# S5 stage of a two-block kernel: turned states kept on their rows, table tiles of 64 rows, decays and U factors made one by one

## The chip, the cores and the metric

The kernel runs on one core of one Trainium2 chip. The metric is device time in microseconds (us) of one execution, as the median of several runs. The profile is one execution of the same program, recorded by the hardware; its times are us from the start of the span unless they are marked ns.

## The reference

Two blocks follow each other on 512 tokens of 1024 features: a block of a convolution and pooling mixer ("even") and a gated linear recurrence ("odd"), then a block of an S5 state-space mixer, an MLP, a gated projection and windowed attention. The part at hand is the S5 mixer. Each of 64 groups has 16 channels and 64 complex states:

```python
a = exp((lam_re + i lam_im) * dt)                      # per group and state
x[t] = a * x[t-1] + B u[t]                             # complex recurrence
y[t] = Re(C x[t]) + d * u[t]                           # C c_re, c_im
y = gelu(y);  ab = y @ w_glu;  out = ab[:, :1024] * sigmoid(ab[:, 1024:])
```

## The kernel before

The S5 mixer works on 64 chunks of 8 tokens. Inside a chunk everything is matrix products with tables; between chunks there is a scan over 64 columns. The features lie in eight tiles (`ft` 0 to 7) of eight groups each.

**Tables.** `tables` makes four tables for each tile while the even stage runs (80 to 430 us), a piece at each `tick`, and writes them to DRAM: `tS` (inputs to states), `tO` (states to outputs), `tM` (inputs to outputs inside a chunk) and `tR` (cosine C and sine N of the rotation of each chunk). `stored` (L1076 to L1080) puts `tO` out with four transfers of 64 rows on SP's queue for each of 16 half tiles.

**odd_out** (L813) ends the odd stage. For each of eight feature tiles it adds the residual (DVE), turns the columns (ACT, `r`), sends them through DRAM by two transfers on POOL's queue into `U`, and then makes two squares (ACT) that are added up (DVE) for two norms.

**s5** (L1165). `enter(ft)` loads the tables S, O, M0, `rotations` loads R; all on SP's queue. `fillers(n)` are blocks of an independent projection, six matmuls of 512 columns each, that are put between; `FILL` says how many stand at which place: four blocks, then the column sums of the squares (`columns`, L368), two blocks, then a chain of small DVE operations (reciprocal square root, three Newton steps, `sel`), 16 small matmuls (L1208) that spread the factor, and one block. Then four decay tiles `dec` (128x512) are made on POOL, U of tiles 0 and 1 is multiplied by the factor on DVE, and U of tiles 2 to 7 on POOL.

- `states(ft)`: 16 matmuls S by U into the PSUM bank `sp` (L1262, 128 rows by 64 columns, two instructions each), then on DVE: multiply by C (512 wide), by N (two of 256), add and subtract (two of 256), two scans of 256 (L1277), multiply by C again (512), by N again (two of 256), a small memset, and four operations on 64 rows by 252 that put real and imaginary part of the turned states `e` on other rows.
- `leave(ft)`: for each of the eight groups, two matmuls M by U (L1302) and two matmuls O by e (L1304), each 128 rows by 64 columns; Gelu on ACT, a round trip through DRAM (`dy`, `yc`), and the split into two halves for the matmuls of `glu`.

The order on PE is the order of the program: states(1) is issued before leave(0), and so on: leave(ft), one block, states(ft+2). From tile 5 on, after each leave, two pieces (`part`, three matmuls each) of the first GLU products follow. `with self.after()` ties a block behind the last instruction of PE issued so far; DVE's states are tied one behind the other (`SEQ`). On the other engines a planner sets the order by a simulated timeline. The weights of `glu` come as `raw` by SP's queue into two buffers, are split by ACT (`hi`) and DVE (`lo`); two of them use the buffers `x` and `gt` that S and M0 leave.

All of tt/mul/add/sub is L252, activation L249, scalar_tensor_tensor L264, tensor_scalar L267, the three matmuls of a product L308 to L310.

Of the kernel before, what the change touches and what calls it, by code (L numbers as in the profile page):

```python
# [11 lines left out]
AF = mybir.ActivationFunctionType  # L12
ALU = mybir.AluOpType
# [155 lines left out]
class Kern:  # L169
# [643 lines left out]
    def odd_out(self, m, o, h):  # L813

        n = self.H("h3")
        v = lambda a: a.rearrange("p (c s) -> p s c", s=8)
        self.add(n.rearrange("p (s c) -> p s c", s=8), v(o), v(h))
        if len(self.tab):


            r = self.L("xc", 2 + self.LAG)
            self.act(r.rearrange("p (s c) -> p s c", s=8), n.rearrange("p (s c) -> p s c", s=8)[:, ::-1], AF.Copy)
            du = self.dram.tile([128, T], F32, name=f"du{m}")
            self.nc.gpsimd.dma_start(out=du.rearrange("(s h) (g c) -> h g s c", s=8, g=8).rearrange("h g s c -> (h g) s c"),
                                     in_=r.rearrange("p (s c) -> p s c", s=8))
            U = self.p_xg.tile([128, 8, 64], F32, tag="xg", name="U")
            self.nc.gpsimd.dma_start(out=U.rearrange("p g c -> p (g c)"), in_=du)
            self.U.append(U)

            for k, g in enumerate((1.0, self.V("g_fin1", m))):  # L830
                q = self.L(*(self.sq if m else ("acc", 2)))
                self.act(q, n, AF.Square, scale=g)
                if m == 0:
                    self.acc12.append(q)
                else:
                    self.add(self.acc12[k], self.acc12[k], q)
        return n


# [142 lines left out]
    def tables(self, small):  # L982

        nc = self.nc
# [16 lines left out]
        for ft in range(8):  # L1001
            eng, eng2 = nc.vector if ft % 2 else nc.gpsimd, nc.gpsimd
            tS, tO, tM, tR = (self.dram.tile([p, w], F32, name=f"{n}{ft}")
                              for n, p, w in (("tS", 128, 1024), ("tO", 128, 1024), ("tM", 128, 256), ("tR", 128, 512)))
# [11 lines left out]
            for q in range(2):  # L1016
# [58 lines left out]

                def stored(q=q, orr=orr, oi=oi, tO=tO):  # L1076
                    for k, w in enumerate((orr, oi)):
                        for g2 in range(2):
                            nc.sync.dma_start(out=tO[64 * k:64 * k + 64, 512 * q:512 * q + 512].rearrange("n (a g m) -> n g a m", a=2, g=2)[:, g2],
                                              in_=w[64 * g2:64 * g2 + 64].rearrange("p a j h -> p a (j h)"))  # L1080

                late(stored)
                if q == 1:
                    def inside(ft=ft, kt=kt, tM=tM):
# [18 lines left out]
            for q in range(2):  # L1103
# [5 lines left out]
                rt = self.L("tq_rt", 2, F32, (128, 2, 128))  # L1109
# [48 lines left out]
            self.queue_w(self.I["w_glu"][m], 8)  # L1158
            self.queue_w(self.I["w_glu"][8 + m], 8)

    GLAG, FILL, AHEAD = 5, (4, 2, 1, 3, 1, 1, 1, 1, 1, 1), 1
    B0P = B1P = ()
    SEQ = 1

    def s5(self, h, fill, glu):  # L1165
        nc = self.nc
        U = self.U
# [60 lines left out]
        with self.tc.high_priority(offset=1500):  # L1228
# [8 lines left out]
            rt = self.L("xc", 2 + self.LAG)[:, 0:64]  # L1237
            self.act(rt, rb, AF.Copy)
        fillers(self.FILL[2])
        self.dec, self.sps, self.yps = [], [], []  # L1240
        for k in range(4):
            dec = self.L("xc", 2 + self.LAG).rearrange("p (a c) -> p a c", a=8)
            self.tt(dec, self.not0.unsqueeze(1).to_broadcast([128, 8, 64]),
                    self.m8[:, 8 * k:8 * k + 8].unsqueeze(2).to_broadcast([128, 8, 64]), ALU.mult, nc.gpsimd)
            self.dec += [dec[:, 0:4], dec[:, 4:8]]
        r8 = rt.unsqueeze(1).to_broadcast([128, 8, 64])
        for ft in range(8):
            self.mul(U[ft], U[ft], r8, nc.gpsimd if ft > 1 else None)
        f4 = lambda: self.L("xs", 2 + 2 * self.LAG).rearrange("p (r a c) -> p r a c", r=2, a=4)

        def states(ft):
            S, O, M = live[ft]
            R, dec, u = Rs[ft], self.dec[ft], U[ft]

            self.sps.append(self.bank("sp"))
            sp = self.sps[-1].rearrange("p (r a c) -> p r a c", r=2, a=4)
            with self.after():

                for a4 in range(4):
                    for r in range(2):  # L1260
                        for g in (2 * a4, 2 * a4 + 1):
                            nc.tensor.matmul(sp[64 * (g % 2):64 * (g % 2) + 64, r, g // 2, :], S[:, r, 64 * g:64 * g + 64], u[:, g, :], start=True, stop=True)  # L1262
            C, N = (R[:, k].rearrange("p (a c) -> p a c", a=4) for k in range(2))
            c2 = C.unsqueeze(1).to_broadcast([128, 2, 4, 64])
            a, b = f4(), f4()
            if ft and self.SEQ:
                with self.tc.issue_after(live["dve"]):
                    self.tt(a, sp, c2, ALU.mult)
            else:
                self.tt(a, sp, c2, ALU.mult)  # L1270
            self.mul(b[:, 0], sp[:, 1], N)
            self.mul(b[:, 1], sp[:, 0], N)
            self.add(a[:, 0], a[:, 0], b[:, 0])
            self.sub(a[:, 1], a[:, 1], b[:, 1])
            for r in range(2):
                z = a[:, r].rearrange("p a c -> p (a c)")
                nc.vector.tensor_tensor_scan(out=z, data0=dec.rearrange("p a c -> p (a c)"), data1=z, initial=0.0, op0=ALU.mult, op1=ALU.add)  # L1277


            e, c = f4(), f4()  # L1280
            self.tt(c, a, c2, ALU.mult)
            self.mul(b[:, 0], a[:, 1], N, nc.gpsimd if ft in self.B0P else None)
            self.mul(b[:, 1], a[:, 0], N, nc.gpsimd if ft in self.B1P else None)
            nc.vector.memset(e[:, :, :, 0:1], 0.0)
            for r, op in ((1, ALU.add), (0, ALU.subtract)):
                for q in range(2):
                    rows = slice(64 * q, 64 * q + 64)
                    self.tt(e[64 * r:64 * r + 64, q, :, 1:64], c[rows, r, :, 0:63], b[rows, r, :, 0:63], op)
            live[ft] = O, M, u, e

        def leave(ft):
            O, M, u, e = live.pop(ft)

            y = self.L("xr", self.XR).rearrange("p (g c) -> p g c", g=8)
            for q in range(2):
                self.yps.append(self.bank("yp"))
                yp = self.yps[-1][:, 0:256].rearrange("p (a c) -> p a c", a=4)
                for a4 in range(4):
                    g = 2 * a4 + q
                    os = [yp[64 * f:64 * f + 64, a4, :] for f in range(2)]  # L1300
                    for f, o in enumerate(os):
                        nc.tensor.matmul(o, M[:, 128 * g + 64 * f:128 * g + 64 * f + 64], u[:, g, :], start=True, stop=False)  # L1302
                    for f, o in enumerate(os):
                        nc.tensor.matmul(o, O[g // 4][:, g % 4, 64 * f:64 * f + 64], e[:, q, a4, :], start=False, stop=True)  # L1304
                self.act(y.rearrange("p (a q) c -> p a q c", q=2)[:, :, q, :], yp, AF.Gelu_apprx_tanh)
            dy = self.dram.tile([128, T], F32, name=f"dy{ft}")
            nc.scalar.dma_start(out=dy, in_=y.rearrange("p g c -> p (g c)"))
            yc = self.L("acc", 2)
            nc.sync.dma_start(out=yc.rearrange("p (s c) -> p s c", s=8),
                                in_=dy.rearrange("(s h) (g c) -> h g s c", s=8, g=8).rearrange("h g s c -> (h g) s c"))  # L1310
            hi, lo = self.LR("y", 24)
            if ft < 6:
                nc.gpsimd.tensor_copy(out=hi, in_=yc)
                self.sub(lo, yc, hi.bitcast(F32), nc.gpsimd)
                ys.append((hi, lo))
            else:
                ys.append(self.split(yc, (hi, lo)))
# [10 lines left out]
        def advance(ft):  # L1328
            states(ft)
            live["dve"] = [i for i in nc.cur_bb.bb.instructions if i.engine == mybir.EngineType.DVE][-1]  # L1330
# [510 lines left out]
```

## Time and profile before

| what | value |
|---|---|
| median of 3 runs | 1881.22 us (1877.48 to 1883.32) |
| profiled execution | 1881.62 us, its span 1879.8 us |
| PE busy | 1760.4 us (94%) |
| DVE, ACT, POOL busy | 1165.6, 762.7, 466.9 us |
| S5 stage proper | about 704 to 785 us |

The view by stretches shows for each engine how long it was busy in a stretch, and the granted clock of TensorE as a share of 2.4 GHz. The timeline shows instructions in order of their start, merged where equal ones follow each other; the difference between two starts is what an instruction really takes of its engine, since matmuls and DVE operations overlap a little. In square brackets stands how long the engine had been idle, and what ended it.

### The profile page before, as it was taken

How to read it: one execution, taken by the hardware profiler on the slowest of the kernel's cores; microseconds unless marked ns; L12 is line 12 of the kernel's file. 1: busy time of each engine (PE TensorE's matmuls, PEld its weight loads, DVE VectorE, ACT ScalarE, POOL GpSimd, SP SyncE). 2: the span in 40 equal slices, each digit the busy share in tenths (PEclk: the TensorE clock that was granted, in tenths of full speed). 3: DMA queues.
4: the chain of work that ended last, by engine and by line, in shares of the span. 5: the costliest groups of instructions: out<-in, count | busy, mean ns of one | idle time of the engine just before them, and what ended most of it. 6: DMA issues, size and time to landing. Idle time of an engine off the chain costs nothing.

```text
span 1879.8 us, 24662 instructions
## 1 busy us (share of the span) xinstructions
PE 1760.4 (94%) x9298; PEld 1440.0 (77%) x9298; DVE 1165.6 (62%) x1885; ACT 762.7 (41%) x1330; POOL 466.9 (25%) x422
## 2 busy tenths in 40 slices
PE   7898999999977896799999999998999999999997
PEld 5776787877755675688888888887778888888886
DVE  9986778756787769555432344578686642244456
ACT  4433443534545362234432342335665432233234
POOL 5552577634666543200000000032000000000002
PEclk8898999999988998899999999999999999999998
DMA  4687344332212488523233223233111233322322
GB/s 164 154 229 194 117 135 124 117 115 68 85 65 93 126 260 276 162 101 107 91 99 101 90 100 98 93 107 112 39 55 49 97 101 93 98 101 92 99 95 91
DMA packets 129015, 216.00 MB, mean 115 GB/s; under 512 B 40064, under 2 KB 79872, under 8 KB 128896
## 3 DMA queue, kind: packets, MB, share of 16 engines
q1 hardware_dynamic: 108144, 189.27, 32.4%
q10 hardware_dynamic: 18112, 16.50, 2.7%
q0 software_dynamic: 2640, 8.65, 1.4%
q8 instruction: 73, 1.20, 0.3%
q14 instruction: 46, 0.38, 0.1%
HBM read 187.97 MB, written 26.28 MB: 114 GB/s over the span
## 4 chain that ended last, share of the span: by engine, by line
PE 69%; DVE 16%; DMA 4%; ACT 3%; POOL 3%; issue 3%; SPq 0%; ACTq 0%; DVEq 0%; POOLq 0%
PE mm L308 20%; PE mm L310 20%; PE mm L309 20%; POOL lo L252 2%; DVE xs L252 1%; DVE lo L252 1%; DVE e L808 1%; PE pv L1620 1%; ACT hi L249 1%; PE sc L309 1%; PE sc L308 1%; PE sc L310 1%; DVE h L264 1%; ACT L249 1%; DVE pl L264 1%
## 5 line engine op out<-in xcount | busy, mean ns | idle before, releaser
L249 ACT ACTIVATE hi<-raw 128x1024 fp32r<-128x1024 f32 (+1 forms) x280 | 292.5, 1046 | 683.9 <-PE mm L309 544.7
L252 DVE TENSOR_TENSOR lo<-raw,hi 128x1024 fp32r<-128x1024 f32 (+1 forms) x211 | 262.6, 1245 | 420.7 <-ACT hi L249 411.4
L310 PE MATMUL mm<-xg,lo 128*128 128x512 f32 x924 | 361.3, 391 | 5.2 <-POOL lo L252 5.2
L308 PE MATMUL mm<-xg,hi 128*128 128x512 f32 x924 | 363.5, 395 | 2.0 <-ACT xs L249 1.5
L309 PE MATMUL mm<-xg,hi 128*128 128x512 f32 x924 | 361.3, 391 | 0.0
L1434 POOL DMA_DIRECT2D pj<-proj x16 | 8.7, 547 | 1026.0 <-DVE t L264 784.0
L308 PE MATMUL mm<-hid,hi 128*128 128x512 f32 (+1 forms) x648 | 250.7, 387 | 1.8 <-DVE t L252 1.8
L309 PE MATMUL mm<-hid,hi 128*128 128x512 f32 (+1 forms) x648 | 250.3, 387 | 0.0
L310 PE MATMUL mm<-hid,lo 128*128 128x512 f32 (+1 forms) x648 | 250.1, 386 | 0.0
L252 POOL TENSOR_TENSOR lo<-raw,hi 128x1024 fp32r<-128x1024 f32 (+1 forms) x69 | 172.1, 2496 | 162.9 <-ACT hi L249 159.7
L310 PEld LDWEIGHTS mm<-xg,lo 128*128 128x128 f32 x924 | 174.3, 189 | 43.2 <-POOL lo L252 6.5
L308 PEld LDWEIGHTS mm<-xg,hi 128*128 128x128 f32 x924 | 174.2, 189 | 42.1 <-issue 2.2
L309 PEld LDWEIGHTS mm<-xg,hi 128*128 128x128 f32 x924 | 174.4, 189 | 35.9 <-DVE xg L252 0.8
L308 PEld LDWEIGHTS mm<-hid,hi 128*128 128x128 f32 x648 | 121.7, 188 | 26.5 <-DVE t L252 2.0
L310 PEld LDWEIGHTS mm<-hid,lo 128*128 128x128 f32 x648 | 121.7, 188 | 24.8
L309 PEld LDWEIGHTS mm<-hid,hi 128*128 128x128 f32 x648 | 121.7, 188 | 24.5
L308 PE MATMUL mm<-y,hi 128*128 128x512 f32 x192 | 78.5, 409 | 10.9 <-ACT y L249 8.0
L310 PE MATMUL mm<-y,lo 128*128 128x512 f32 x192 | 76.9, 401 | 1.2 <-POOL lo L252 1.2
L309 PE MATMUL mm<-y,hi 128*128 128x512 f32 x192 | 76.7, 399 | 0.0
L309 PE MATMUL mm<-big,hi 128*128 128x512 f32 x160 | 64.8, 405 | 4.6 <-DVE big L264 4.6
L310 PE MATMUL mm<-big,lo 128*128 128x512 f32 x160 | 64.7, 405 | 3.8 <-DVE lo L252 3.3
L308 PE MATMUL mm<-big,hi 128*128 128x512 f32 x160 | 65.3, 411 | 0.9 <-ACT hi L249 0.9
(467 smaller groups left out, 3090.8 us busy)
## 6 DMA issues: line engine op xcount, KB each, us to landing
raw<-in_w_up SPq DMA_DIRECT2D x64, 512.0 KB
raw<-in_w_down SPq DMA_DIRECT2D x64, 512.0 KB
raw<-in_w_in_even SPq DMA_DIRECT2D x40, 512.0 KB
raw<-in_w_in_odd SPq DMA_DIRECT2D x24, 512.0 KB
raw<-in_w_out_even SPq DMA_DIRECT2D x16, 512.0 KB
raw<-in_w_glu SPq DMA_DIRECT2D x16, 512.0 KB
raw<-in_w_gate SPq DMA_DIRECT2D x16, 512.0 KB
raw<-in_w_out_odd SPq DMA_DIRECT2D x16, 384.0 KB
```

The lines of the kernel that those rows point to most:

```text
L249: self.nc.scalar.activation(out=out, in_=in_, func=func, scale=scale, bias=bias)
L252: (eng or self.nc.vector).tensor_tensor(out=out, in0=a, in1=b, op=op)
L264: self.nc.vector.scalar_tensor_tensor(out=out, in0=a, scalar=s, in1=b, op0=op0, op1=op1)
L308: mm(out, hi[:, sl], xh, start=start, stop=False)
L309: mm(out, hi[:, sl], xl, start=False, stop=False)
L310: mm(out, lo[:, sl], xh, start=False, stop=stop)
L808: nc.vector.tensor_tensor_scan(out=y, data0=u[:, k], data1=x[:, k], initial=0.0, op0=ALU.mult, op1=ALU.add)
L1434: self.nc.gpsimd.dma_start(out=p, in_=pj[m])
L1620: mm(o, l, r[:, w], start=n == 0, stop=n == 6 * nk - 1)
```

## The change

Five edits:

1. In `states` the second N product is made negative (scalar_tensor_tensor with -1), so that one addition of 512 replaces an addition and a subtraction of 256. After the scans the same is done, and one addition of 128 rows by 504 replaces the four operations on 64 rows; `e` now keeps real and imaginary part in its columns, and the two groups of a pair on its rows.
2. `leave` takes O from 64-row tiles: instead of two matmuls of 128 rows for each group there are four of 64 rows (real and imaginary part, two column halves), with a tile position.
3. `stored` writes `tO` in the new layout: two transfers of 128 rows instead of four of 64.
4. Only the first decay tile is made ahead; the other three stand between the U multiplications on POOL; U of tile 1 goes from DVE to POOL.
5. `odd_out` makes the squares before the turning and its transfers; one of the four blocks ahead of the column sums is moved behind them.

```diff
@@ odd_out
         if len(self.tab):
+            for k, g in enumerate((1.0, self.V("g_fin1", m))):
+                q = self.L(*(self.sq if m else ("acc", 2)))
+                self.act(q, n, AF.Square, scale=g)
+                ...
             r = self.L("xc", 2 + self.LAG)
             self.act(r..., AF.Copy)
             ...
             self.U.append(U)
-            for k, g in enumerate((1.0, self.V("g_fin1", m))):
-                ...
@@ tables / stored
                     for k, w in enumerate((orr, oi)):
-                        for g2 in range(2):
-                            nc.sync.dma_start(out=tO[64 * k:64 * k + 64, 512 * q:512 * q + 512].rearrange("n (a g m) -> n g a m", a=2, g=2)[:, g2],
-                                              in_=w[64 * g2:64 * g2 + 64].rearrange("p a j h -> p a (j h)"))
+                        nc.sync.dma_start(out=tO[:, 512 * k + 256 * q:512 * k + 256 * q + 256], in_=w.rearrange("p a j h -> p (a j h)"))
@@
-    GLAG, FILL, AHEAD = 5, (4, 2, 1, 3, 1, 1, 1, 1, 1, 1), 1
+    GLAG, FILL, AHEAD = 5, (3, 3, 1, 3, 1, 1, 1, 1, 1, 1), 1
@@ s5
-        for k in range(4):
+        def decay(k):
             ...
+        decay(0)
         for ft in range(8):
-            self.mul(U[ft], U[ft], r8, nc.gpsimd if ft > 1 else None)
+            with self.after(mybir.EngineType.Pool) if ft > 1 else nullcontext():
+                self.mul(U[ft], U[ft], r8, nc.gpsimd if ft else None)
+                if ft in (2, 4, 6):
+                    decay(ft // 2)
@@ states
             self.mul(b[:, 0], sp[:, 1], N)
-            self.mul(b[:, 1], sp[:, 0], N)
-            self.add(a[:, 0], a[:, 0], b[:, 0])
-            self.sub(a[:, 1], a[:, 1], b[:, 1])
+            self.stt(b[:, 1], sp[:, 0], -1.0, N, ALU.mult, ALU.mult)
+            self.add(a, a, b)
...
-            self.mul(b[:, 0], a[:, 1], N, nc.gpsimd if ft in self.B0P else None)
-            self.mul(b[:, 1], a[:, 0], N, nc.gpsimd if ft in self.B1P else None)
+            self.stt(b[:, 0], a[:, 1], -1.0, N, ALU.mult, ALU.mult)
+            self.mul(b[:, 1], a[:, 0], N)
             nc.vector.memset(e[:, :, :, 0:1], 0.0)
-            for r, op in ((1, ALU.add), (0, ALU.subtract)):
-                for q in range(2):
-                    rows = slice(64 * q, 64 * q + 64)
-                    self.tt(e[64 * r:64 * r + 64, q, :, 1:64], c[rows, r, :, 0:63], b[rows, r, :, 0:63], op)
+            self.add(e[:, :, :, 1:64], c[:, :, :, 0:63], b[:, :, :, 0:63])
@@ leave
-                    for f, o in enumerate(os):
-                        nc.tensor.matmul(o, O[g // 4][:, g % 4, 64 * f:64 * f + 64], e[:, q, a4, :], start=False, stop=True)
+                    rows = slice(64 * q, 64 * q + 64)
+                    for r in range(2):
+                        for f, o in enumerate(os):
+                            nc.tensor.matmul(o, O[r][rows, a4, 64 * f:64 * f + 64], e[rows, r, a4, :], start=False, stop=r == 1, tile_position=(64 * q, 64 * f))
```

## Rows read from the trace of the kernel before

**Rows 1.** Busy time by stretch (busy us, instructions), granted clock, DMA share, GB/s.
```profile
713.32:772.10 58.78, 38.38 (x641) 32.07 (x641) 55.34 (x109) 16.12 (x27) 16.19 (x15) 0.88 0.77 249
```

**Rows 2.** Timeline of PE, 708 to 724: start, us, line, operation, [idle before].
```profile
708.71 0.46 PE L1208 MATMUL st<-ctile,xc 128*32 128x64 f32 x16 [3.89 <-DVE xc L252]
...
711.29 1.98 PE L1262 MATMUL sp<-U,x 128*64 128x64 f32 x32
...
723.73 0.48 PE L1304 MATMUL yp<-xs,i 128*64 128x64 f32 x4 [4.81 <-DVE xs L252]
```

**Rows 3.** Timeline of DVE, 702 to 718: the chain of small operations, U, the first states.
```profile
702.68 0.15 DVE L267 TENSOR_SCALAR st_s<-st 128x4 f32<-128x4 f32 x1
...
703.27 2.76 DVE L267 TENSOR_SCALAR st_s<-st_s 128x4 f32<-128x4 f32 x1
...
709.49 3.06 DVE L252 TENSOR_TENSOR U<-U,xc 128x512 f32<-128x512 f32 x2 [0.93 <-ACT xc L249]
...
714.59 2.07 DVE L252 TENSOR_TENSOR xs<-xs 128x256 f32<-128x256 f32 x2
716.58 3.38 DVE L1277 TENSOR_TENSOR_SCAN xs<-xc,xs 128x256 f32<-128x256 f32 x2
```

**Rows 4.** Timeline of POOL, 702 to 720: decays and U.
```profile
702.95 3.05 POOL L252 TENSOR_TENSOR xc<-ctile,m 128x512 f32<-128x512 f32 x3
...
710.29 9.12 POOL L252 TENSOR_TENSOR U<-U,xc 128x512 f32<-128x512 f32 x6
```

**Rows 5.** Timeline of DVE, 724 to 731: the states of one tile with POOL idle.
```profile
724.15 1.35 DVE L252 TENSOR_TENSOR xs<-sp,y 128x512 f32<-128x512 f32 x3
725.43 0.75 DVE L252 TENSOR_TENSOR xs<-xs 128x256 f32<-128x256 f32 x2
726.09 1.27 DVE L1277 TENSOR_TENSOR_SCAN xs<-xc,xs 128x256 f32<-128x256 f32 x2
...
728.65 1.74 DVE L252 TENSOR_TENSOR xs<-xs 64x252 f32<-64x252 f32 x4
730.42 1.35 DVE L252 TENSOR_TENSOR xs<-sp,y 128x512 f32<-128x512 f32 x3
```

**Rows 6.** Timeline of PE, 728 to 732: states of tile 2 and leave of tile 1.
```profile
727.96 0.39 PE L309 MATMUL mm<-y,hi 128*128 128x512 f32 x1
728.18 0.39 PE L310 MATMUL mm<-y,lo 128*128 128x512 f32 x1
728.50 1.15 PE L1262 MATMUL sp<-U,x 128*64 128x64 f32 x32
729.48 0.40 PE L1302 MATMUL yp<-U,gt 128*64 128x64 f32 x8
...
730.16 0.29 PE L1302 MATMUL yp<-U,gt 128*64 128x64 f32 x4
730.28 0.29 PE L1304 MATMUL yp<-xs,O 128*64 128x64 f32 x4
...
731.78 0.50 PE L308 MATMUL mm<-y,hi 128*128 128x512 f32 x1
```

**Rows 7.** Timeline of PE in the attention stage, 1345: 128-row and 64-row matmuls in turn.
```profile
1345.58 0.39 PE L1562 MATMUL sc<-mask,idb 128*128 128x512 bf16 x1
1345.90 0.38 PE L1566 MATMUL sc<-k,q 64*128 64x256 f32 x1
```

**Rows 8.** Timelines of PE, SP and ACT, 764 to 785: the late wait and its sources.
```profile
772.11 0.80 PE L308 MATMUL mm<-y,hi 128*128 128x512 f32 x1 [7.98 <-ACT y L249]
...
784.95 0.50 PE L308 MATMUL mm<-y,hi 128*128 128x512 f32 x1
...
764.90 0.33 SPq L288 DMA_DIRECT2D raw<-in_w_glu  x1
...
770.51 1.06 ACT L249 ACTIVATE hi<-raw 128x1024 fp32r<-128x1024 f32 x1 [7.47 <-DMA raw<-in_w_glu]
```

**Rows 9.** The tile tq_wr: what POOL and DVE waited for before writing it.
```profile
  DMA tO<-tq_wr: 7.2, 4
```

More of the change, by code (lines that the diff above doesn't have):

```diff
@@ L818, in odd_out @@
         if len(self.tab):
+            for k, g in enumerate((1.0, self.V("g_fin1", m))):
+                q = self.L(*(self.sq if m else ("acc", 2)))
+                self.act(q, n, AF.Square, scale=g)
+                if m == 0:
+                    self.acc12.append(q)
+                else:
+                    self.add(self.acc12[k], self.acc12[k], q)
             r = self.L("xc", 2 + self.LAG)
@@ L828, in odd_out @@
             self.U.append(U)
-            for k, g in enumerate((1.0, self.V("g_fin1", m))):
[L831 to L836, printed above, removed]
         return n
@@ L1240, in s5 @@
         self.dec, self.sps, self.yps = [], [], []
-        for k in range(4):
+        r8 = rt.unsqueeze(1).to_broadcast([128, 8, 64])
+        def decay(k):
             dec = self.L("xc", 2 + self.LAG).rearrange("p (a c) -> p a c", a=8)
@@ L1245, in s5 @@
             self.dec += [dec[:, 0:4], dec[:, 4:8]]
-        r8 = rt.unsqueeze(1).to_broadcast([128, 8, 64])
+        decay(0)
         for ft in range(8):
-            self.mul(U[ft], U[ft], r8, nc.gpsimd if ft > 1 else None)
+            with self.after(mybir.EngineType.Pool) if ft > 1 else nullcontext():
+                self.mul(U[ft], U[ft], r8, nc.gpsimd if ft else None)
+                if ft in (2, 4, 6):
+                    decay(ft // 2)
         f4 = lambda: self.L("xs", 2 + 2 * self.LAG).rearrange("p (r a c) -> p r a c", r=2, a=4)
```

## The prediction

> **What bounds the kernel now.** I read the page first: PE is busy for 94% of the span, so only stretches where PE waits or runs slowly can be won. The list of PE's waits puts the S5 stage among the worst, and the view by stretches shows it: from 713 to 772 us PE is busy for 38.4 of 58.8 us, DVE for 55.3, at a granted clock of 0.88 [rows 1]. The timelines of the single engines then show who is late. There are four places. (1) After the column sums PE stands still for 3.89 us behind DVE's chain of small operations [rows 2]. (2) The first leave waits 4.81 us for the first states [rows 2]. (3) After that each tile goes at DVE's pace, 6.27 us (724.15 to 730.42, start to start) when POOL is idle [rows 5], while PE's own work for a tile is less (below). (4) At 764 PE waits 7.98 us for ACT, which stands behind a weight transfer [rows 8]. From 772 on PE hardly stops: whatever is to be won must be won before, and all that is added to PE after is paid in full.
>
> **Edit 4 and 5, the head of the stage.** The chain of small operations runs from 702.68 to PE's start at 708.71, 6.0 us, and one 128x4 operation of it takes 2.76 us where its neighbour takes 0.15 [rows 2, 3]; just then POOL makes three decays, 702.95 to 706.0 [rows 4]. With one decay ahead this stretch goes: 3.4 us remain. The column sums stand one block, six matmuls of 0.22 [rows 6], or 1.4 us, earlier; blocks in all are the same, so PE is free at 704.8 as now. The chain thus starts between 701.3 and 702.7 (if the weight split that stands before it on DVE keeps its place) and frees PE between 704.8 and 706.1. I take 705.3: 3.4 us won, bounds 2.6 and 3.9. The squares going first costs U's last transfer two squares of ACT, some 1.2 us; U of tile 7 isn't wanted for 50 us more, so nothing, and without that cover 1.2. U of tile 0 is no longer followed by one on DVE, but its first took 709.49 to 711.29, 1.8 us, beside a decay; between 0.66 (two clean operations of 256 [rows 5]) and 1.8 I take 1.2, 0.6 won. The first 32 state matmuls took 1.98 us after PE's wait, those of tile 2 1.15 [rows 2, 6]; 0.8 won, as PE hardly stops. So states(0) on DVE starts about 4.8 us earlier, at 708.5.
>
> There it meets POOL, which now has seven U and three decays behind the factor: 7 x 1.52 + 3 x 1.02 [rows 4] = 13.7 us, to about 719.5. With POOL busy, the two 256-wide operations took 2.07 instead of 0.75 and the two scans 3.38 instead of 1.27 [rows 3, 5]: 0.66 and 1.05 more for each. Seven operations of the new states(0) read two SBUF inputs: 5 x 0.66 + 2 x 1.05 = 5.4, on top of 5.2: done at 719.1, leave(0) 4.6 us earlier than 723.7. Bounds: nothing met (leave(0) 9 us earlier, where PE itself is the limit), and a whole POOL operation of 1.52 ahead of each of the seven, 10.6 instead of 5.4 (0.6 later than now). I take the measured delays, which were met beside the same U operations. The Trainium skill (SBUF — State Buffer, Who interferes with whom) says that a DVE operation with two SBUF inputs and a GpSimd one that reads SBUF shut each other out for the whole instruction. The scans' 1.05 fall short of a whole 1.52; by that rule taken strictly the sum is the dearer of the two bounds.
>
> **Edit 1, DVE for each tile.** Of the 6.27 us, the add and subtract take 0.66 (725.43 to 726.09) and the four 64-row operations 1.77 (728.65 to 730.42) [rows 5]. One operation of 512 isn't dearer than the pair of 256 that it replaces, nor is one of 504: 0.66 each, down to half of that. So 6.27 - 1.77 + 0.66 = 5.2, 1.1 less for each tile, 8.9 for eight. The negating form costs what the multiplication does (both stream 256 from the same places).
>
> **Edit 2, PE for each tile.** Four instructions (two column tiles side by side) go every 0.12 us [rows 6]. A leave has 64 of them now, 1.9 us; the 64-row tiles add 32, that is 0.94. Then the changes of tile shape. From the 512-column matmul at 728.18 to the first state matmul 0.32 pass, of which 0.22 are its own; the 32 state matmuls take 0.98 instead of 8 x 0.117: a change from 128x128 to 128x64 costs 0.09 + 0.05 = 0.14 [rows 6]. In attention, from 128 to 64 rows, the same gap stands: 0.32 after a 512-column matmul [rows 7]. Now M (128x64) and O (128x64) have one shape. After, O is 64x64 and M isn't, and they alternate: two M ahead, then O, M, ... with O of the fourth and fifth group together, 13 changes in a leave. No row has just this change; bounds are 0 (no drain between these two) and 0.2 (0.10 on either side); I take 0.14, the nearest row in width: 1.8 us. Leave: 1.9 + 0.94 + 1.8 = 4.7 (2.8 if free, 5.4 at the dear end). The Trainium skill (TensorEngine Tiling (Array Packing), Tiling Modes) says that changing the mode, not merely the tile, drains TensorE, and lists 128x64 and 64x64 as two modes. It speaks against this edit: by it a leave isn't 2.8 but the 4.7 taken here, and the rows show such a gap wherever the shape changes.
>
> A tile on PE is then 1.12 (states, with their entry) + 4.7 + 0.2 (way back) + 1.4 (block) = 7.3 us; it was 4.6. DVE wants 5.2, and up to 1.4 more where POOL splits y. **PE becomes the bound of the stage**, at a pace slower than DVE's old one; what the head wins is handed back tile by tile.
>
> **Sum.** leave(0) at 719.1 runs its first 3 us at the half clock, after a wait as long as now: 1.5 more. It ends at 719.1 + 4.4 + 1.5 = 725.0, its block at 726.6. Five tiles of 7.3: 763.3. The spread in tile 4, eight small matmuls, 1.2: 764.5. Then two GLU pieces 1.4, states(7) 1.1, leave(6) 4.9, pieces 1.4, leave(7) 4.9, pieces 1.4: 779.6. By then 18 GLU matmuls are done; now PE has done 22 of them by 784.95 [rows 8] (28 on the timeline from 761.5 on, six of them a block): 0.9 more, 780.5. Without the late wait: 4.5 us won.
>
> The late wait. ACT turns a weight (hi) whose transfer is issued at 764.90 and lands 5.6 us later, and an eviction that frees a PSUM bank stands behind it; PE goes on at 772.11 [rows 8]. The transfer waits for a raw buffer, that for DVE's lo into gt, and gt for the last M of leave(5). In the new run leave(5) ends near 762.9, not earlier than now (761.5): lo 1.5, transfer 5.6, hi 1.06, eviction 0.6 bring PE to 771.7 again. After it stand 15.4 us of work (as above, with the 0.9) and some 3 us for the half clock, as now: 790, 5.0 later. Whether the eviction still stands behind hi is the planner's order, which no row shows; half and half gives +0.3.
>
> **Edit 3.** tO goes out in 32 transfers instead of 64, on SP's queue where weights stand too. Waits for them are 7.2 us in four [rows 9], on POOL and DVE, not on PE; at most a part reaches PE: 0 to 3, I take 1.
>
> Total +0.3 - 1.0 = -0.7 on the profiled 1881.62 (span 1879.8 and 1.8 around it, 0.4 above the median): 1881, its own range 1876 to 1887.
>
> **Rivals.**
> - *The change of shape is free.* For: no row has 128x64 against 64x64, and weights are loaded ahead. Against: [rows 6, 7] show a gap at every other change. A tile is then 5.5 on PE, and DVE's 5.2 to 6.6 sets the pace, say 5.8: seven times 1.5, some 10.5 less; with or without the late wait 1866 to 1876, about 1870.
> - *Slower: the late wait stays, and PE pays twice.* ACT's eviction stays behind hi as it is now; leave(5) is no earlier, so PE stops at 765 and the two last leaves, 2.8 us longer each, lie behind the wait. It decides if the eviction is planned after hi: +5.0 - 1.0, and on top of that either the dear bound of the first states (up to 5.2 later, and the wait with them) or 0.2 for each of the 26 changes behind the wait (1.6): 1886 to 1891, about 1888.
> - *The head isn't won*, since DVE's weight split stands before the chain: 1 us less, inside the range.
>
> **Chances.** PE bound, wins and losses near balance: 0.47. Free change of shape: 0.30. Late wait with full price: 0.23. About 0.3%, 5.6 us, is what a measurement of this kernel can tell from no change. Faster: 0.30 x 0.9 + 0.47 x 0.15 = 0.34. Slower: 0.23 x 0.75 + 0.47 x 0.12 = 0.23. Same: 0.43. Cases of both signs are in it; the range for 8 in 10 reaches from the free change to most of the slower case: 1868 to 1889.
>
> **What would show it.** PE's small operation of 2.76 us gone and L1208 near 705; leave(0) near 719; a step of 0.14 at each change between L1302 and the O matmuls and a leave of 4.7 us; PE without waits for DVE between 727 and 763, DVE waiting for sp; one wait near 765 or none. I am wrong if leaves take under 3.5 us, if DVE still has no gap, or if the planner moves other work.

## The result and the profile after

| | before | after |
|---|---|---|
| median of six runs each, us | 1882.4 (1877.5 to 1885.7) | 1892.3 (1890.0 to 1896.0) |
| ratio, 95% interval | | 1.0057 (1.0039 to 1.0074) |
| profiled execution: its time, its span, us | 1881.6, 1879.8 | 1890.9, 1889.0 |
| first state matmuls on PE, start | 711.29 | 707.00 |
| first leave (O matmuls), start | 723.73 | 725.77 |
| first tanh of the GLU (the stage's work is nearly done) | 803.99 | 816.30 |

The change makes the kernel slower by 0.57%, 9.9 us, 3 us above the top of the forecast range. The head of the stage was won as forecast, and lost again before the first leave. PE's waits from 700 to 820 (what waited, for whom, sum, times, longest), first those of before, then those of after:

```profile
PE yp L1304 <- DVE xs L252: 12.3, 4, 4.8
PE mm L308 <- ACT y L249: 8.0, 1, 8.0
PE st L1208 <- DVE xc L252: 3.9, 1, 3.9
```

```profile
PE yp L1308 <- DVE xs L252: 12.0, 1, 12.0
PE st L1206 <- DVE xc L252: 0.7, 1, 0.7
```

The wait for the chain of small operations went from 3.89 to 0.73, and the one for ACT's late eviction, 7.98, is gone. The leaves' four waits for states have become one, for the first states: 11.98 where the first of the four was 4.81. DVE's timeline of after shows what stood in its way, and POOL's what was going on there:

```profile
708.20 1.02 DVE L252 TENSOR_TENSOR xs<-sp,y 128x512 f32<-128x512 f32 x2 [1.70 <-PE sp L1267]
709.13 0.41 DVE L264 SCALAR_TENSOR_TENSOR xs<-sp,y 128x256 f32<-128x256 f32 x1
709.58 11.65 DVE L252 TENSOR_TENSOR xs<-xs 128x512 f32<-128x512 f32 x1
721.34 1.27 DVE L1281 TENSOR_TENSOR_SCAN xs<-xc,xs 128x256 f32<-128x256 f32 x2
722.53 1.20 DVE L252 TENSOR_TENSOR lo<-raw,hi 128x1024 fp32r<-128x1024 f32 x1
```

```profile
707.47 0.55 POOL L835 DMA_DIRECT2D U<-du  x1 [6.91 <-DMA du<-xc]
708.03 1.06 POOL L252 TENSOR_TENSOR xc<-ctile,m 128x512 f32<-128x512 f32 x1
709.04 2.54 POOL L252 TENSOR_TENSOR U<-U,xc 128x512 f32<-128x512 f32 x2
...
718.43 1.03 POOL L252 TENSOR_TENSOR xc<-ctile,m 128x512 f32<-128x512 f32 x1
719.43 1.25 POOL L252 TENSOR_TENSOR U<-U,xc 128x512 f32<-128x512 f32 x1
```

The one addition that replaces the add and the subtract takes 11.65 us; the next one of its form takes 0.69. It ends 0.55 us after POOL's last U (720.68). POOL works without a pause from its DMA issue at 707.47 on, each U at 1.25 us, not slowed at all (1.52 in [rows 4]). The three operations ahead of it, which read sp, took 1.02 (two of them) and 0.41 us beside POOL's first decay, as in later tiles with POOL idle.

From the first leave to the first tanh, the rows of before and of after (stretch; length, then busy time of PE, weight loads, DVE, ACT, POOL with counts; granted clock, DMA share, GB/s):

```profile
723.73:803.99 80.26, 64.67 (x846) 54.03 (x847) 55.68 (x113) 17.20 (x32) 14.00 (x12) 0.87 0.56 172
```

```profile
725.77:816.30 90.53, 90.53 (x1110) 71.10 (x1111) 44.36 (x84) 17.29 (x31) 14.07 (x12) 0.89 0.50 155
```

PE stood idle for 15.6 us of this stretch before and does not now: 90.53 of 90.53 us busy. It is the bound, as forecast, but its stretch is 10 us longer than the 80.4 of my sum without the late wait. Part of that is the clock. The same stretch of after in pieces:

```profile
725.77:742.00 16.23, 16.23 (x223) 12.58 (x224) 10.14 (x22) 1.31 (x4) 0.00 (x0) 0.69 0.51 170
742.00:749.00 7.00, 7.00 (x126) 5.46 (x125) 4.93 (x9) 2.16 (x4) 2.73 (x2) 1.00 0.81 231
749.00:757.00 8.00, 8.00 (x126) 6.21 (x122) 5.00 (x11) 1.36 (x3) 2.10 (x2) 0.79 0.72 231
757.00:772.00 15.00, 15.00 (x256) 11.98 (x252) 9.82 (x22) 4.98 (x9) 4.28 (x4) 1.00 0.78 242
772.00:781.00 9.00, 9.00 (x84) 6.76 (x82) 4.40 (x8) 2.28 (x4) 2.21 (x2) 0.62 0.70 198
781.00:816.30 35.30, 35.30 (x316) 28.11 (x312) 10.08 (x16) 5.20 (x9) 2.74 (x2) 1.00 0.22 68
```

Three stretches lie partly at the half clock (1.2 of 2.4 GHz): one behind the long wait, two with PE busy all the time. As an estimate, busy time by clock, 90.53 x 0.89, is 80.6 us of work at full clock, and 9.9 us are the clock's. The same working on the row of before gives 64.67 x 0.87 = 56.3 us of work and 8.4 for the clock, beside the 15.6 idle. So against before this stretch has some 24 us more work for PE, 15.6 us less idle time and 1.5 us more for the clock: eight leaves of 5.1 instead of 1.9 us cost PE more than the waits that they could fill.

### The profile page after: what moved, and what is told of

It reads as the page before. It is cut to its first block, busy times and chain, and to the rows that moved or that the text cites. A ratio compares the mean times of both kernels' runs of the same rounds, so it can differ in the third digit from the quotient of the medians.

```text
span 1889.0 us, 25099 instructions
## 1 busy us (share of the span) xinstructions
PE 1779.0 (94%) x9554; PEld 1449.1 (77%) x9554; DVE 1151.7 (61%) x1852; ACT 762.5 (40%) x1330; POOL 463.5 (25%) x423
## 4 chain that ended last, share of the span: by engine, by line
PE 72%; DVE 15%; ACT 3%; DMA 3%; issue 3%; POOL 3%; SPq 0%; ACTq 0%; DVEq 0%; POOLq 0%
PE mm L308 20%; PE mm L310 20%; PE mm L309 20%; POOL lo L252 1%; PE yp L1308 1%; DVE e L808 1%; DVE xs L252 1%; DVE lo L252 1%; DVE h L264 1%; PE pv L1624 1%; PE yp L1303 1%; ACT hi L249 1%; DMA raw<-in_w_in_odd 1%; PE sc L308 1%; DVE t L264 1%
```

## The experiments

Theory A: the loss comes from POOL's train of operations, which kept the addition waiting. Theory B: it is PE's price for the 64-row tiles, and whatever the head wins comes back as a wait. The first four experiments part them.

**Take POOL out of the head.** U of all tiles and decays 1 to 3 on DVE:

```diff
@@ s5, in decay(k)
-                    ... ALU.mult, nc.gpsimd)
+                    ... ALU.mult, None if k else nc.gpsimd)
@@ s5
-        for ft in range(8):
-            with self.after(mybir.EngineType.Pool) if ft > 1 else nullcontext():
-                self.mul(U[ft], U[ft], r8, nc.gpsimd if ft else None)
-                if ft in (2, 4, 6):
-                    decay(ft // 2)
+        for ft in range(2):
+            self.mul(U[ft], U[ft], r8)
@@ advance, behind the states of tile ft
+            if ft + 2 < 8:
+                with self.tc.issue_after(live["dve"]):
+                    self.mul(U[ft + 2], U[ft + 2], r8)
+                    if ft % 2 == 0:
+                        decay(ft // 2 + 1)
+                ...
```

> The changed kernel with the U factors of all tiles and decays 1 to 3 on VectorE (U of tiles 0 and 1 ahead of the first states, each later one behind the states two tiles before); GpSimd does nothing in the head of the stage but the first decay. Theory A (the loss is GpSimd's train of operations, which kept one VectorE addition waiting for 11 us): that addition takes 0.69 us instead of 11.65, the first leave starts near 714.5 instead of 725.8, the last leave ends near 786 instead of 797, VectorE's tile of 4.9 + 0.69 + 0.35 = 5.9 us stays below TensorE's 7.5, time 1880 us (1877 to 1884). Theory B (the loss is TensorE's price for 64-row tiles, whatever the head does): the won time returns as a wait for a weight near 765, time 1887 or more.

Measured: 1880.1 us, ratio 0.9992 (0.9981 to 1.0003). The addition takes 0.69, the first leave starts at 716.87, 8.9 us earlier than in after (2.4 later than I expected), with a wait of 1.0. The win didn't come back as a wait: those of PE up to 820 sum to 4.0 us, and the stretch from the first leave to the first tanh is

```profile
716.87:802.46 85.59, 85.03 (x1110) 67.19 (x1111) 55.24 (x93) 18.75 (x34) 14.79 (x12) 0.96 0.62 194
```

The same 1110 instructions as in after, at 0.96 instead of 0.89: 4.9 us less. Theory A holds for the wait. The clock is a second part; that it comes with the wait isn't shown, as the next kernel tells.

**The wide addition, or any operation?** Only the addition in two of 256 again:

```diff
-            self.add(a, a, b)
+            self.add(a[:, 0], a[:, 0], b[:, 0]); self.add(a[:, 1], a[:, 1], b[:, 1])
```

> The changed kernel, only the one 512-wide addition ahead of the scans is made in two of 256 again; GpSimd's train stays. Theory A1 (the wide one-piece addition is what GpSimd's train keeps out): the two take 0.6 to 1.5 us each as in the kernel before, the first leave starts near 719 as forecast, time 1885 us. Theory A2 (anything that comes into the midst of the train with two SBUF inputs stands until the train ends): the first of the two takes some 11 us, the first leave starts near 726, time 1891 us, no change against the changed kernel.

Measured: 1892.9 us, 1.0061 (1.0044 to 1.0079). Here another operation stood, the multiplication of U of tile 0, even before the first states (DVE, then POOL's head of the train):

```profile
703.62 13.49 DVE L252 TENSOR_TENSOR U<-U,xc 128x512 f32<-128x512 f32 x1 [0.93 <-ACT xc L249]
```

```profile
703.42 0.55 POOL L835 DMA_DIRECT2D U<-du  x1 [7.08 <-DMA du<-xc]
703.99 1.06 POOL L252 TENSOR_TENSOR xc<-ctile,m 128x512 f32<-128x512 f32 x1
704.99 2.48 POOL L252 TENSOR_TENSOR U<-U,xc 128x512 f32<-128x512 f32 x2
```

The two additions came only after the train and took 0.75 us together, so this run says nothing on their form; that follows from the head alone, below. It shows that the addition isn't special: the first DVE operation with two SBUF inputs that meets the train is kept. This one began 0.37 us ahead of POOL's first decay, but 0.20 behind its DMA issue. PE's long wait, 12.3 us, now lies ahead of the first state matmuls, and the leave comes without one. The stretch from there to the first tanh, in a trace of this kernel's fastest execution (1888.5 us):

```profile
726.60:811.55 84.95, 84.95 (x1114) 67.19 (x1111) 46.72 (x91) 18.20 (x32) 13.59 (x12) 0.96 0.56 174
```

The leaves run at 0.96 here too, with U on POOL and a wait of 12 us some microseconds before them.

**The price of a change of shape.** The same matmuls, in each half of a leave the eight M first, then the sixteen O, 3 changes of shape in a leave instead of 15. (The matmuls of a half now form one PSUM group for each column tile: `start` only at the first M, `stop` at the last O.)

```diff
+                ...
                 for a4 in range(4):
                     g = 2 * a4 + q
                     for f in range(2):
-                        nc.tensor.matmul(o, M[:, 128 * g + 64 * f:128 * g + 64 * f + 64], u[:, g, :], start=True, stop=False)
+                        nc.tensor.matmul(os[a4][f], M[:, 128 * g + 64 * f:128 * g + 64 * f + 64], u[:, g, :], start=a4 == 0, stop=False)
+                for a4 in range(4):
                     for r in range(2):
                         for f in range(2):
-                            nc.tensor.matmul(o, O[r][rows, a4, 64 * f:64 * f + 64], e[rows, r, a4, :], start=False, stop=r == 1, tile_position=(64 * q, 64 * f))
+                            nc.tensor.matmul(os[a4][f], O[r][rows, a4, 64 * f:64 * f + 64], e[rows, r, a4, :], start=False, stop=r == 1 and a4 == 3, tile_position=(64 * q, 64 * f))
```

> The changed kernel with the same matmuls in another order: in each half of a leave the eight M matmuls first, then the sixteen 64-row O matmuls, so that the tile shape changes 3 times in a leave instead of 15. Head unchanged: first leave near 725.8. If the change of shape is the price (0.147 us each, from 0.645 us a group where the matmuls alone are 0.35): a leave at full clock takes 5.1 - 12 x 0.147 = 3.3 us, TensorE's tile 5.8, time 1879 to 1884 us, the lower end if no wait for a weight comes back. If the price is that of 64-row matmuls themselves: a leave stays near 5 us and the time near 1891.

Measured: 1883.9 us, 1.0008 (0.9996 to 1.0020). A leave at full clock, first here, then in after (PE):

```profile
734.13 0.64 PE L1304 MATMUL yp<-U,gt 128*64 128x64 f32 x16
734.70 1.15 PE L1308 MATMUL yp<-xs,O 64*64 64x64 f32 x32
735.77 0.69 PE L1304 MATMUL yp<-U,gt 128*64 128x64 f32 x16
736.39 1.15 PE L1308 MATMUL yp<-xs,O 64*64 64x64 f32 x32
737.47 0.50 PE L308 MATMUL mm<-y,hi 128*128 128x512 f32 x1
```

```profile
736.63 0.28 PE L1303 MATMUL yp<-U,gt 128*64 128x64 f32 x4
736.84 0.45 PE L1308 MATMUL yp<-xs,O 64*64 64x64 f32 x8
737.22 0.34 PE L1303 MATMUL yp<-U,gt 128*64 128x64 f32 x4
...
741.35 0.45 PE L1308 MATMUL yp<-xs,O 64*64 64x64 f32 x8
741.73 0.50 PE L308 MATMUL mm<-y,hi 128*128 128x512 f32 x1
```

3.34 against 5.10 us with the same instructions: 1.76 for 12 changes, 0.147 each. That M and O take turns on one PSUM region is not what costs: in before they do so with one shape, and four instructions still go every 0.12 us [rows 6]. Eight leaves would give 14.1 us; the medians differ by 8.4, in part because a late wait is back:

```profile
PE mm L308 <- ACT y L249: 4.7, 1, 4.7
```

In after PE has no wait there; that PE comes to the place only when the weight is there is the likely reason.

**The head alone.** Old tables, states and leaves, new decays, U, squares and blocks (edits 4 and 5).

> The kernel before with the new head alone (one decay ahead, the others between the U factors on GpSimd, squares first, one block moved); old tables, old states on VectorE, old leave without 64-row tiles. Theory A2 (any VectorE operation with two SBUF inputs stands until GpSimd's train ends): first leave near 726, 2 us later than before, tiles at VectorE's old 6.3 us, time 1881 to 1885. Theory A1 (only the wide addition stood): first leave near 719, time 1876 to 1880. Theory B (all of the loss is TensorE's price): time 1881 or less, since that price is gone.

Measured: 1884.1 us, 1.0011 (0.9997 to 1.0026); first leave at 724.61 behind a wait of 13.2 us. The pair of 256-wide operations stood behind the same train:

```profile
707.07 12.58 DVE L252 TENSOR_TENSOR xs<-xs 128x256 f32<-128x256 f32 x2
```

Theory A2: the old form of the addition is kept as well. The head's edits alone don't win.

**Why did DVE stand here, when it took turns with POOL before?** In the kernel before, POOL's six U ran beside DVE's U, additions and scans, and both got on [rows 3, 4]. All the trains that kept DVE out have one thing in common: POOL issued a DMA just ahead, and no pause lay between. There is such a train in before too. The row of POOL ahead of the three decays:

```profile
702.38 0.55 POOL L827 DMA_DIRECT2D U<-du  x1 [4.48 <-DMA du<-xc]
```

The 2.76-us operation of [rows 3] started at 703.27 and ended at 706.03, when the last of the decays had ended [rows 4]: it stood for the rest of the train, not for one operation. (This 128x4 operation has a single SBUF input, so two inputs aren't the whole rule. In the kernel with the layout alone, below, it stands for 3.00 us behind the same three decays, led in the same way.)

The rest of the fourteen traces, from their starts to their ends, bears the lead out. Each has about 30 other trains of three or more tensor_tensor operations on POOL without a pause of over 0.15 us, the longest of 45 (315.75 to 349.29 in before), none led by a DMA issue; some of them began when a transfer landed (ten operations from 282.43 in after, behind a wait of 1.2 us), so it isn't the landing either. Beside them no DVE operation takes over 2.3 us more than the shortest of its form. One train in each trace with a DMA issue ahead kept nobody: four memsets, which read nothing (1293.73 to 1298.25 in after, beside eight DVE operations in 6.02 us).

The next two experiments break the lead in two ways. First, a pause behind the DMA issue: POOL's U read a copy of the factor row that DVE makes just before its addition (the added lines stand in a function that is called there for tile 0 only; U of tile 0 stays ahead, on DVE).

```diff
@@ s5, in states(0) just ahead of self.add(a, a, b)
+            nc.vector.tensor_copy(out=rt2, in_=rt)
+            r8 = rt2.unsqueeze(1).to_broadcast([128, 8, 64])
+            for ft in range(1, 8):
+                with self.after(mybir.EngineType.Pool) if ft > 1 else nullcontext():
+                    self.mul(U[ft], U[ft], r8, nc.gpsimd)
+                    if ft in (2, 4, 6):
+                        decay(ft // 2)
```

> The changed kernel, but GpSimd's seven U factors and three decays read a copy of the factor row that VectorE makes just before its 512-wide addition; so GpSimd pauses after its DMA issue and the first decay, and the train starts anew without a DMA issue at its head. Theory D (a train that begins with a DMA issue of GpSimd keeps VectorE out until it ends; one without it lets VectorE in between two operations): the addition takes 0.7 to 1.9 us, the scans a microsecond more each, the first leave starts at 719 to 721, time 1884 to 1888 us. Theory T (any train without pauses keeps it out): the addition takes some 11 us again, the first leave starts at 726 to 727, time 1891 to 1893 us.

Second, the DMA itself elsewhere: that of U of tile 7 is issued ahead of the last U.

```diff
@@ odd_out
-            self.nc.gpsimd.dma_start(out=U.rearrange("p g c -> p (g c)"), in_=du)
+            if m < 7:
+                self.nc.gpsimd.dma_start(out=U.rearrange("p g c -> p (g c)"), in_=du)
+            else:
+                self.du7 = du
@@ s5
+                if ft == 7:
+                    nc.gpsimd.dma_start(out=U[7].rearrange("p g c -> p (g c)"), in_=self.du7)
                 self.mul(U[ft], U[ft], r8, nc.gpsimd if ft else None)
```

> The changed kernel, but the transfer that brings in U of tile 7 is issued by GpSimd ahead of the last U operation, not ahead of the first decay: the same train, without the DMA issue at its head. Theory D: VectorE gets in between GpSimd's operations, none of its own takes over 2 us before the DMA issue comes, the first leave starts at 716 to 720, time 1882 to 1887 us. Theory T: U of tile 0 or the addition stands 9 us or more until the train has ended near 718 to 720, the first leave starts at 723 or later, time 1889 us or more.

> The kernel with the transfer of U of tile 7 issued late, once more, for a second trace: its profiled run was 9 us faster than the median of its runs. Theory D: VectorE gets in between GpSimd's operations again, no operation of the first states over 2 us, first leave near 719; a longer run then shows a lower granted clock on TensorE (0.961 to 0.964 instead of 0.968), that is longer stretches at the half clock, 8 us or more in sum. Theory T: an operation of 9 us or more stands in the longer runs.

DVE and POOL of the kernel with the DMA issued late:

```profile
704.06 0.69 DVE L252 TENSOR_TENSOR U<-U,xc 128x512 f32<-128x512 f32 x1 [1.17 <-ACT xc L249]
706.20 1.03 DVE L252 TENSOR_TENSOR xs<-sp,y 128x512 f32<-128x512 f32 x2 [1.45 <-PE sp L1272]
707.14 0.42 DVE L264 SCALAR_TENSOR_TENSOR xs<-sp,y 128x256 f32<-128x256 f32 x1
707.59 1.10 DVE L252 TENSOR_TENSOR xs<-xs 128x512 f32<-128x512 f32 x1
708.79 3.22 DVE L1286 TENSOR_TENSOR_SCAN xs<-xc,xs 128x256 f32<-128x256 f32 x2
711.93 1.99 DVE L252 TENSOR_TENSOR lo<-raw,hi 128x1024 fp32r<-128x1024 f32 x1
713.85 3.15 DVE L252 TENSOR_TENSOR xs<-xs,y 128x256 f32<-128x256 f32 x2
716.92 1.26 DVE L264 SCALAR_TENSOR_TENSOR xs<-xs,y 128x256 f32<-128x256 f32 x1
```

```profile
704.10 3.03 POOL L252 TENSOR_TENSOR U<-U,xc 128x512 f32<-128x512 f32 x2 [4.01 <-ACT xc L249]
707.10 1.04 POOL L252 TENSOR_TENSOR xc<-ctile,m 128x512 f32<-128x512 f32 x1
708.11 3.35 POOL L252 TENSOR_TENSOR U<-U,xc 128x512 f32<-128x512 f32 x2
...
717.85 0.59 POOL L1255 DMA_DIRECT2D U<-du  x1
```

The same operations of POOL without a pause, no DMA issue at their head, and the two engines take turns: no DVE operation over 2 us, POOL's U stretched from 1.25 to 1.7 on average. U of tile 0 began 0.04 us ahead of POOL's first operation and took 0.69; in the kernel with the split addition, 0.37 ahead of it but behind the DMA issue, it took 13.49. The first leave starts at 718.95, in the second trace of this kernel at 722.81, where the whole head came 4.1 us later; counted from the first state matmuls that is 13.9 and 13.7 us (18.8 in after). With the pause DVE takes turns as well (addition 0.69, the two scans 3.23), though the train starts later there and the first leave starts at 724.99. Theory D by the mechanism in all three traces. By the time only in part: 1891.2 (1.0041) with the pause and 1891.1 (1.0031; 1.0012 to 1.0050) with the DMA late, above the 1884 to 1888 and 1882 to 1887 that I expected, and not clear of the changed kernel's 1.0057 (1.0039 to 1.0074). The time of the late-DMA kernel follows its clock: 1879.5 and 1881.7 us in the runs at a mean granted clock of 0.967 and 0.968, 1887 to 1897 in the ten at 0.959 to 0.966. Its second trace has 0.87 from the first leave to the first tanh, the first one 0.91. So the expectation of the second trace on the clock held too.

**Both parts, each way.** The layout alone, as it would be without the new head (edits 1 to 3):

> The kernel before with the new tables, the new states on VectorE and the 64-row tiles alone; decays, U, squares and blocks as before. If TensorE's price for the 64-row tiles is a loss by itself: first leave near 722 (the two small additions and the four 64-row ones are fewer), TensorE's tile 7.5 us, last leave near 793, time 1885 to 1890 us. If only the new head is the loss: VectorE's faster tiles are won, time 1881 us or less.

Measured: 1889.8 us, 1.0041 (1.0020 to 1.0061): a loss by itself. The trace is of an execution at 1898.0 us, and its head is late (first leave at 728.91, not near 722), but PE has no gap from the first leave to the first tanh:

```profile
728.91:820.92 92.01, 92.01 (x1110) 72.58 (x1111) 48.18 (x84) 17.30 (x31) 13.55 (x12) 0.87 0.50 153
```

So theory B's price is real as well; only that it swallows whatever the head wins was wrong. Then both remedies, grouped leaves and U and all decays on DVE:

> The changed kernel with both remedies: U and all decays on VectorE, spread over the tiles, and each half of a leave with its M matmuls first and the O matmuls behind them. Theory A with the price of 0.147 us for a change of shape: first leave near 716, leaves of 3.3 us, TensorE's tile 5.8 and VectorE's 5.9 us, time 1869 to 1877 us, the upper half if the wait for a weight near 765 comes back (4.7 us in the grouped kernel). Theory B (the won time only comes back as a wait): 1880 us, no better than with one remedy.

Measured: 1877.5 us, **0.9964 (0.9953 to 0.9975)**, just above the 1869 to 1877 that I expected. PE's waits tell where the rest went:

```profile
PE mm L308 <- ACT y L249: 8.2, 3, 4.3
PE sp L1264 <- DMA x<-tS: 4.4, 1, 4.4
PE yp L1301 <- ACT xr L249: 1.7, 1, 1.7
```

Now that PE is early, weights and tables are late. Grouped leaves with the DMA issued late, U left on POOL:

> Grouped leaves and the transfer issued late, U and decays still on GpSimd in one train. If the first states only pay for taking turns (7 us, as in the kernel with the transfer issued late) and TensorE's price is gone: first leave near 719, leaves of 3.3 us, time 1876 to 1881 us, up to 3 above the kernel with both remedies, since a wait for a weight near 765 stands in both. If the way the train is led decides nothing in time: 1884 us, as the grouped kernel alone.

Measured: 1880.2 us, 0.9972 (0.9959 to 0.9985). And the old layout with the new head and the DMA issued late:

> Old tables, states and leaves with the new head, the transfer of U of tile 7 issued late. Theory D: no operation of the first states over 2 us, first leave near 720 instead of 724.6, VectorE's tiles at 6.3 us, the late wait near 765 shortened or not: time 1878 to 1883 us, 1 to 5 below the new head alone. Theory T: an operation of 9 us or more stands, first leave near 724, time 1884 us.

Measured: 1877.7 us, **0.9964 (0.9951 to 0.9978)**; no operation of the first states over 2 us, first leave at 717.78. The ratios to before, in one table:

| leaves | DMA issue leads POOL's train | DMA issued late | U on DVE |
|---|---|---|---|
| old, 128 rows | 1.0011 | 0.9964 | not tried |
| 64 rows, M and O in turn | 1.0057 (the change) | 1.0031 | 0.9992 |
| 64 rows, grouped | 1.0008 | 0.9972 | 0.9964 |

By these ratios each row gains 5 to 9 us from one DMA issue, and each column 5 to 11 from the order of the 64-row matmuls. The weak one is the middle row, the change itself: its two intervals overlap, and the medians, 1892.3 and 1891.1, differ by 1.2 us only. With both mended the new layout is as fast as the old one, not faster.

**Does the wait bring the half clock?** Four blocks moved into PE's wait:

```diff
-    GLAG, FILL, AHEAD = 5, (3, 3, 1, 3, 1, 1, 1, 1, 1, 1), 1
+    GLAG, FILL, AHEAD = 5, (3, 3, 1, 7, 0, 0, 0, 0, 1, 1), 1
```

> The changed kernel, with four blocks (six 512-column matmuls each, 1.4 us at full clock) that stand behind the first four leaves moved ahead of the states of tile 1, into TensorE's wait of 12 us; the number of blocks stays 16. Theory C1 (the stretches at half clock behind the first leave, about 8 us in the changed kernel, follow the long wait): the wait shrinks to about 6.5 us, the first leave and what follows run mostly at full clock (granted 0.95 or more from the first leave to the first tanh), time 1878 to 1882 us. Theory C2 (they follow the small matmuls of the leaves): the clock there stays at 0.86 to 0.91, only the 5.6 us of blocks are won, time 1885 to 1887 us. Theory C3 (the blocks' weights aren't there yet): TensorE waits in the moved blocks instead, time 1888 us or more.

Measured: 1895.6 us, 1.0067 (1.0043 to 1.0090), none of the three as they stood. The wait shrank to 3.9, and 2.5 are now waited for an eviction inside the moved blocks. The first O matmuls came at full clock, for 0.5 us; then PE ran at the half clock up to 736. From the first leave to the first tanh:

```profile
728.10:813.59 85.49, 84.72 (x1090) 68.19 (x1091) 48.08 (x84) 13.94 (x26) 13.64 (x12) 0.88 0.50 153
```

0.88, with four blocks of 512 columns fewer between the leaves, and a mean clock of 0.954 to 0.965 in its twelve runs. C1 falls: a wait cut to 3.9 us doesn't bring the clock back. The clock part of C2 fits, its time doesn't; C3's time fits, but PE waited for an eviction there and not for weights.

## Why the prediction was wrong, step by step

Right: the head. The 2.76-us operation is gone, the selection matmuls start at 705.02 (forecast 705.3), the first state matmuls at 707.00 run at full clock, states(0) starts at 708.20 on DVE (708.5). Right: DVE's tile (5.35, back to back from 725.63; forecast 5.2), PE as the bound without a gap, and the gap at a change of shape (0.147; 0.14). The rival that this change is free is refuted by the grouped leaves. The Trainium skill (TensorEngine Tiling (Array Packing), Tiling Modes) states that a change of mode drains TensorE; the 0.147 us agree with it.

Two steps failed: the price of the first states' meeting with POOL, by its mechanism, and the term for the half clock, by its size. In the order of time (first tanh at 816.30, by my sum 803.99 + 0.3 - 1.0 = 803.3):

- **The meeting with POOL, +6.7.** I priced seven operations at the delays of operations that took turns, 5.4 us in all. The same rows held the other case, an operation that stood for three of POOL's [rows 3, 4], and I counted it only as a gain where it went. Edit 4 moves three decays in between the U, so that the train is eleven operations long, and its first decay comes right behind the issue of U's last transfer, at 707.47. The dear bound, 10.6, is near what happened (10.96 more for the one addition), but by luck: it was thought of as seven turns of one POOL operation each, not as one turn of a whole train. Besides, taking turns was priced too low as well: the kernel with the DMA issued late needs 12.75 us from the first state operation to the leave, not 10.6, with 1.0 more instead of 0.66 for each multiplication and a weight split of 2.0 in the middle that my sum left out. The late DMA brought the first leave 6.8 us forward in its trace, but the median only by 1.2, so this step alone doesn't explain the time.
- **The clock, +8.4.** I took 1.5 us for the half clock behind the wait; 9.9 were paid. All of leave(0) and its block ran at it, and two later stretches without a wait before them. My sum built the stretch from steps at full clock, though the row of before has 0.87 there, 8.4 us by the same estimate. What sets these stretches stays open.
- **Leaves, +1.7.** 80.6 us of work at full clock against 78.9: 15 changes of shape instead of 13, 5.1 instead of 4.7 for a leave.
- **The late wait, -4.8.** I took half of it. It didn't come, and the likely reason is not the planner's order of ACT but that PE was too late to meet it. It came back at 4.7 and 4.9 us in the two kernels whose leaves are grouped and whose U are on POOL, and as 8.2 in three waits with both remedies.
- **Edit 3, +1.0.** The waits behind these transfers went from 7.2 to 5.0 us [rows 9]. It wasn't tried alone, and nothing behind the head shows it; whatever it brought before lies in the start of the head, which came 0.3 us earlier than forecast.

The sum is +13.0. Behind the first tanh 1072.7 us follow, before 1075.8, 3.1 less; what made these I can't tell from the clock's scatter. That gives the 9.9 us by which the profiled execution lies above the forecast. The slower rival had the right sign and the wrong mechanism: no late wait, but its side condition, the dear bound of the first states.

The Trainium skill (SBUF — State Buffer, Who interferes with whom) says that the loser of the shared ports stands for the whole instruction of the other. The operations that read sp went on beside POOL (1.02 and 0.41 us, as alone), as it says for those with one SBUF input outside the two-port modes. In the kernels led by a DMA issue the loser stood for a whole train (11.65 us), which goes further than the page.

## What to carry to other kernels

When work moves to POOL beside a chain of DVE operations with two SBUF inputs, look not only at the price of a meeting but at what leads POOL's train: in these kernels a DMA issue directly ahead of it turned delays of 0.4 to 1.2 us each into one of 11 to 13 us. Issuing that DMA a few operations later was worth 7 to 9 us with the old and the grouped leaves, and 1 to 5, not clear of noise, in the changed kernel. When 64-row tiles are mixed with 128-row ones, count the changes of shape (0.147 us here) and order the matmuls so that there are few. And once PE has no gap left, what is added to it and each stretch at the half clock has no wait left to be hidden in.

## What was not expected of the hardware

- A VectorE operation with two SBUF inputs stood for 11.65, 13.49, 12.35, 11.64 and, in the old form, 12.58 us (two of 256) behind a GpSimd train that a DMA issue led, in all five kernels that have such a train of eleven; behind trains of the same operations with no DMA issue at their head, none over 2.3 us in four kernels. Why the lead matters stays open.
- The granted clock fell to the half level in the middle of stretches where PE was busy all the time (749 to 757 and 772 to 781 in after). The same matmuls ran at 0.96 with U on DVE, but also with U on POOL and the split addition. Filling the wait ahead didn't help (0.88). What decides it stays open.
